# Attention over 32 units: the second softmax scaling of a run issued at the fifth filler product in place of the eighth

## The chip, the core and the metric

The kernel runs on one core of one Trainium2 chip. The metric is device time in microseconds: the median of three executions of the kernel before is 997.88 us (997.6 to 998.34). A second source is one execution taken by the hardware profiler, with its own time and its own span.

## The reference

One layer of a hybrid encoder trunk: RMSNorm, one input projection, two-dimensional neighbourhood attention, a SiLU gate, one output projection with the residual, and a last RMSNorm. The sequence is 2048 tokens, laid out as 32 rows of 64; the width is 1024, in 16 heads of 64.

```python
h = rmsnorm(x, norm_0)
q, k, v, gate = jnp.split(h @ w_in_0, 4, axis=-1)      # 1024 -> 4 * 1024
# for every row r of 64 queries: keys and values of 8 rows, 16 columns around the query
s = jnp.einsum('bnqhd,bknjhd->bhnqkj', qr, kr) * 64 ** -0.5
s = jnp.where(col_valid, s + bias, -1e30)              # bias from rpb_0, per head
p = softmax(s)                                         # over the 8 rows and their columns
o = jnp.einsum('bhnqkj,bknjhd->bnqhd', p, vr)
x = x + (o * silu(gate)) @ w_out_0
out = rmsnorm(x, norm_f)
```

## The kernel before, in words

All matrices are float32. A product of two of them is made of three matmuls on TensorE: each operand is split into a leading part and a rest (`h` and `l` in the names: `hh`, `hl`, `woh`, `wol`, `gh`, `gl`), and the rest-by-rest product is left out. A split is two instructions: ScalarE (ACT) copies the operand to the leading part, then VectorE (DVE) subtracts that from the operand. A **filler product** below is one such matmul of 128x512, three of them for each block of 128 of the contraction.

The kernel has four stages. The first two make the values and most of the queries, keys and gates (seven products for a two-by-two block product, in place of eight). The third is the attention loop, in which all that the change touches stands. The fourth, `rows_by_seven`, makes six pairs of blocks of 128 output rows, again with seven products for a pair; the four blocks that come first are made plainly, by `outputs`, as filler in the loop.

**The loop (L1805).** There are 33 runs, m = 0 to 32. A unit of attention is a pair of heads `p` and a block `T` of eight query rows (512 queries). Run m makes the scores of unit m and finishes unit m - 1. A unit has two halves, of two column groups each: `scores(2m)` and `scores(2m + 1)`. The order of the work is fixed when the program is written out, by hand and by a counter of filler products (`clock`); each engine takes its instructions in that order and waits for semaphores. In one run TensorE (PE) has, in this order:

- filler products, which `feed` takes from the projections that are left (`pp`, L392 to L396) and, from about run 18, from the plain output rows (`po`, L1580 to L1584);
- 44 transposes of the probabilities of unit m - 1 (`turns`, L1357), from the tiles `x` to PSUM tiles `ph`; DVE and ACT copy these, three copies each, to `pta` (L1345, L1347);
- 32 score matmuls of unit m (`scores`, L1297) into PSUM tiles `s`, which can be written only when a PSUM bank has come free: the pool `banks` has eight, all kinds of PSUM tile share them, and nearly all the scores' banks are those that the `ph` copies empty;
- 32 value matmuls of unit m - 1 (`values`, L1376) into `o`.

Behind the scores, DVE adds the bias and takes the row minimum (L1306) and ACT takes the exponential and its sum (L1312). `normalise` then makes the reciprocals of four sums (L1317, DVE) and scales four tiles `x` by them. The first half of a unit is scaled inside `scores(2m + 1)`, by GpSimd (POOL) alone. The **second half is scaled in the next run**, `normalise(2 * m - 1, True, ...)`, so that its exponentials have time: there DVE scales two tiles (L1322), ACT one (L1324) and POOL one (L1326). The transposes read all of them.

Beside this, the loop issues:

- `consume`: the next split of a weight block, of `w_in` or, from about run 12, of `w_out` (L198 and L199: `woh`, `wol`). Before it, it asks for a load some blocks ahead (L171, SyncE's (SP's) queue), and it splits only a block that was asked for at least 36 counts earlier. Its place in a run is with the scaling (`between`) or ahead of the k-th part of the filler, by the run's number;
- `split_rows`: the split of a block of attention output for the plain output rows (L1422, L1423: `gh`, `gl`);
- `give`: what follows the last filler product of a projection's group. A gate's block goes through ACT (L372, tanh) and DVE (L373), `sg<-sg,pp`; a key's goes through ACT (L378);
- `add_rows`: the residual of an output block (L1452, DVE), and five counts later its squares (L1455, ACT, `xr<-y`);
- stores and loads on SP's queue that `store` has put down for a later count (`due`).

The lines in run m that set where the second scaling stands:

```python
a = amount[m] - 8
begin(m)
feed(8)
if m:
    ...
        normalise(2 * m - 1, True)
    ...
    for k in range(3):
        ...                      # split_rows() or consume(1, turn=True), by m and a
        feed(a * 0.2)
else:
    feed(a * 0.6)
feed(a * 0.4, 8 if a > 12 else 4)
if m:
    turns(m - 1)
```

`amount[m]` is 13.5 filler products, 1.5 more or less in runs 8 to 23. The last `feed` also runs on, by up to three products, while an event (a split, the end of a group) is less than 4 or 8 counts old.

Of the kernel before, what the change touches and what calls it, by code (L numbers as in the profile page):

```python
# [77 lines left out]
def build(ctx, tc, x, xr, xt, wg, bias, w_out, n0, nf, out):  # L78
# [191 lines left out]
    for n, (k, j, ph, c) in enumerate(halves):  # L270
        a = (KINDS[k] + j, ph)
# [36 lines left out]
    def consume(n, asked=False, turn=False):  # L308
        for _ in range(n):
            load_ahead()  # L310
            if attending[0] and not asked and not turn:
                return
            if state["used"] == len(items) or not may_use(items[state["used"]]):
                return
            if attending[0] and now() - asked_at[items[state["used"]]] < 36 and not asked:
                return
            it = items[state["used"]]
            state["used"] += 1
            use_item(it)
# [24 lines left out]
    def due(n):  # L344
        clock[0] += n
        while later and later[0][0] <= clock[0]:
            later.pop(0)[2]()
# [848 lines left out]
    def projections():  # L1196
        for n, (kind, j, ph, c) in enumerate(halves):
            state["half"] = n
            w = (KINDS[kind] + j, ph)
            for a in range(2):  # L1200
                if n == len(halves) - 5 and a == 0:
                    for k in range(RES_EARLY):
                        load_res(*turns_[k])
                if n == len(halves) - 1:
                    if a == 0:
                        load_og(0)
                        load_og(1)
                    else:
                        store(("og0",), 9, lambda: split_og(0))
                consume(1)  # L1210
                p = yield from group(w, a, c, n)
                state["event"] = clock[0]
                give(kind, 2 * j + a, c, p, True)
            state["done_halves"] = n + 1
# [100 lines left out]
    def normalise(i, both=False, between=None):  # L1315
        st = ST.pop(i)
        nc.vector.reciprocal(st[:, 8:12], st[:, 4:8])  # L1317
        for j, C in enumerate(pairs[i][2]):
            for s in range(2):
                o = 8 + 2 * j + s  # L1320
                if both and j:
                    nc.vector.tensor_scalar(X[i, C][s], X[i, C][s], st[:, o:o + 1], None, op0=OP.mult)  # L1322
                elif both and s:
                    nc.scalar.activation(X[i, C][s], X[i, C][s], AF.Copy, scale=st[:, o:o + 1])  # L1324
                else:
                    nc.gpsimd.tensor_scalar(X[i, C][s], X[i, C][s], st[:, o:o + 1], 1.0, op0=OP.mult, op1=OP.mult)  # L1326
        if between:
            between()
# [182 lines left out]
    def run_roots(most=99):  # L1511
        while roots and most and (roots[0][0] <= clock[0] or ended[0]):
            most -= 1
            _, n, root, scale, send = roots.pop(0)
            root()
            rooted.append((n, scale, send))

    def run_scales():
        while rooted:
            n, scale, send = rooted.pop(0)  # L1520
            scale()
            store(("y", n), 18, send)
# [7 lines left out]
    def rows_due():  # L1530
        n = ready["split"]
        return (n < ready["loaded"] and "turn" in ready and place[n] <= ready["turn"] + 3 and now() - late["loaded_at"][n] >= 40 \
                and sum(1 if hasattr(g, "rearrange") else 2 for g in G.values()) <= 6)

    def split_rows():
        n = ready["split"]
        if rows_due():
            split_og(n)
            ready["split"] += 1
            return True  # L1540
# [77 lines left out]
    def land_T2():  # L1618
        for f in ("A21", "A22"):
            load_rows_of(1, f, vh)  # L1620
        for m in range(LEADERS):
            load_rest_of(m)
        land([("T2", k, i) for k in range(4) for i in range(2)], [a[k, 1] for k in range(4) for a in (woh, wol)])
        for f in ("A21", "A22"):
            load_rows_of(2, f, qp)
# [11 lines left out]
    def form_rows(m, P):  # L1637
        src = A[m, uses[P][0]]
        F[m, P] = t = wp([128, 2, 512], F32R, "f")
        nc.scalar.activation(t[:, 0], src, AF.Copy)  # L1640
        nc.vector.tensor_tensor(t[:, 1], src, t[:, 0].bitcast(F32), OP.subtract)
# [108 lines left out]
    for m in range(8, 24):  # L1750
        amount[m] += 1.5 if m % 2 == 0 else -1.5
    calm_debt = 3
    amount += [(96 * (12 - len(units_two)) + 48 * PLAIN - sum(amount) - first - end_of_it) / (cycles - 25)] * (cycles - 25) + [end_of_it]
    fill = projections()
    outs = outputs()
# [3 lines left out]
    def feed(n, calm=0):  # L1759
        credit[0] += n  # L1760
        while credit[0] > 0 or credit[0] > -calm_debt and clock[0] - state["event"] < calm:
            if alive[0]:
                got = next(fill, None)
                if got is None:
                    alive[0] = False
                    continue
            else:
                got = next(outs, None)
                if got is None:
                    due(max(credit[0], 0.0))  # L1770
                    credit[0] = min(credit[0], 0.0)
                    return
            credit[0] -= got
            due(got)
# [5 lines left out]
    def all_loads():  # L1780
        while any(e[1][0] == "load" for e in later):
            later.pop(0)[2]()

    def begin(m):
        all_loads()
        quiet[0] = False
        if m >= 1:
            later_loads([lambda: load_sg(*order[m - 1])], 1, 0)
        if m == cycles - 1:
            later_loads([land_first], 1.5, 0)  # L1790
            later_loads([lambda f=f, i=i: load_rows_of(i, f) for i in ((2, 0, 1) if PLAIN <= 6 else (0, 1)) for f in ("A11", "A12")], 10, 0.5)
        if m == cycles:
            later_loads([land_rest], 4, 0)
        if m < cycles:
            later_loads([lambda: load_v(*order[m])], 4, 0)
        if m + 1 < cycles:
            nx = order[m + 1]
            later_loads([load_q(*nx), load_k(*nx)], 7, 5)
            if (nx[0], ROW_TYPE[nx[1]]) not in EM:
                later_loads(load_bias(nx[0], ROW_TYPE[nx[1]]), 3, 1.5)  # L1800
# [4 lines left out]
    for m in range(cycles + 1):  # L1805
        a = amount[m] - 8
        begin(m)
        feed(8)
        if m:
            due_here = []  # L1810
            quiet[0] = True
            if a < 12 and m > 8 and m % 2:
                normalise(2 * m - 1, True, lambda: due_here.append(split_rows() or consume(1, turn=True)))
            else:
                normalise(2 * m - 1, True)
            most, behind = 99 if a > 12 else 0 if rows_due() else 1, bool(rooted)
            run_scales()
            if not (behind or any(due_here)):
                run_roots(most)
            for k in range(3):  # L1820
                if m == 1 and k == 2:
                    pass
                elif a > 12 or not any(due_here) and (k < 1 or k < 2 and m > 8 and m % 2 == 0):
                    got = split_rows()
                    due_here.append(got)
                    if not got:
                        consume(1, turn=True)
                    elif a < 12 and m % 2 == 0 and len(items) - state["used"] == 8:
                        feed(a * 0.2)
                        consume(1, turn=True)  # L1830
                feed(a * 0.2)
        else:
            feed(a * 0.6)
        quiet[0] = False
        feed(a * 0.4, 8 if a > 12 else 4)
        if m:
            turns(m - 1)
        if m == cycles:
            all_loads()
            feed(6)  # L1840
            while next(outs, 0) != 0:
                due(1)
            land_T2()
            for n in range(3):
                form_rows(n, 1)
        else:
            scores(2 * m)
            if m == 0:
                feed(first)
            scores(2 * m + 1, lambda: normalise(2 * m))  # L1850
            if m == 0:
                consume(2, turn=True)
        if m:
            values(m - 1)
        runs[0] += 1
        if m == 8:
            late_loads()
# [37 lines left out]
```

## Time and profile before

| | |
|---|---|
| median of three runs | 997.88 us (997.6 to 998.34) |
| profiled execution, its own time | 998.06 us |
| its span | 996.0 us (2.1 us less than its time) |
| TensorE (PE) busy | 986.9 us, 99% |
| weight loads (PEld) busy | 789.4 us, 79% |
| VectorE (DVE) busy | 772.9 us, 78% |
| ScalarE (ACT) busy | 541.6 us, 54% |
| GpSimd (POOL) busy | 128.5 us, 13% |
| mean granted TensorE clock | 0.999 |

The first transposes of the loop start at 575.28 us of the span (run 1), the last at 871.33 us (run 32). From 875.30 us to the end it is `rows_by_seven`. TensorE is busy all the time by the page, but its matmuls overlap, and a short wait between two of them hardly shows in that row; the time from the first matmul of a block to the first of the next tells it better. Weight loads have a row of their own.

### The profile page before, as it was taken

What the parts mean: (1) busy time and instruction counts of PE and PEld (TensorE: products, weight loads), DVE (VectorE), ACT (ScalarE), POOL (GpSimd) and SP (SyncE); (2) the same over time, 40 slices, a digit from 0 to 9 for tenths busy, and PEclk for the clock granted to TensorE, in tenths of its full rate; (3) what the DMA queues carried; (4) which work ended last, traced back from release to release, by engine and by line L of the source; (5) the groups of instructions that cost most, each with busy time, mean ns of one, the idle gap of its engine ahead of it and who ended that gap; (6) DMA issues with size and microseconds to landing.
All of it is one profiled execution on the core that took longest, in us unless ns stands there. A gap on an engine that the chain in (4) does not pass through costs nothing.

```text
span 996.0 us, 19496 instructions
## 1 busy us (share of the span) xinstructions
PE 986.9 (99%) x6892; PEld 789.4 (79%) x6892; DVE 772.9 (78%) x1703; ACT 541.6 (54%) x1310; POOL 128.5 (13%) x204
## 2 busy tenths in 40 slices
PE   9999999999999999999999999999999999999997
PEld 6888888888888888888888777777776777788886
DVE  5899888987665876766776687788889888886866
ACT  7863245465535442333433377777777786653443
POOL 0000001231100000000000022223232322201110
PEclk9999999999999999999999999999999999999999
DMA  8933547777947846656565798888978787997754
GB/s 285 347 116 104 195 134 255 246 250 251 363 150 222 275 123 194 205 174 213 175 191 195 229 286 270 271 240 261 320 231 290 244 251 236 329 358 199 196 153 116
DMA packets 150120, 227.65 MB, mean 229 GB/s; under 512 B 13640, under 2 KB 65096, under 8 KB 150024
## 3 DMA queue, kind: packets, MB, share of 16 engines
q1 hardware_dynamic: 147000, 221.30, 69.1%
q0 software_dynamic: 2592, 4.72, 2.9%
q8 instruction: 54, 0.88, 0.4%
q10 hardware_dynamic: 432, 0.40, 0.1%
q14 instruction: 42, 0.34, 0.1%
HBM read 160.31 MB, written 66.06 MB: 227 GB/s over the span
## 4 chain that ended last, share of the span: by engine, by line
PE 97%; ACT 1%; DVE 1%; DMA 0%; SPq 0%; issue 0%; POOL 0%; DVEq 0%; POOLq 0%
PE pp L448 40%; PE pv L614 13%; PE py L1674 11%; PE o L1376 8%; PE s L1297 7%; PE ph L1357 4%; PE pp L394 3%; PE pp L396 2%; PE pp L392 2%; PE pv L729 2%; PE po L1582 1%; PE po L1584 1%; PE po L1580 1%; DMA land<-in_xt_dram 0%; ACT x L1312 0%; DVE pta L1345 0%
## 5 line engine op out<-in xcount | busy, mean ns | idle before, releaser
L448 PE MATMUL pp<-h,f 128*128 128x512 f32 x576 | 185.4, 389 | 0.0
L448 PE MATMUL pp<-t,f 128*128 128x512 f32 x702 | 171.3, 389 | 0.0
L448 PEld LDWEIGHTS pp<-t,f 128*128 128x128 f32 x702 | 131.8, 188 | 27.4
L1326 POOL TENSOR_SCALAR x<-x,st 128x360 f32<-128x360 f32 (+5 forms) x160 | 81.8, 527 | 526.2 <-DVE st L1317 526.2
L1312 ACT ACTIVATE x<-x,st 128x360 f32<-128x360 f32 (+5 forms) x256 | 134.2, 526 | 26.9 <-DVE st L1306 26.8
L448 PEld LDWEIGHTS pp<-h,f 128*128 128x128 f32 x576 | 108.1, 188 | 22.5
L448 PE MATMUL pp<-l,f 128*128 128x512 f32 x288 | 112.1, 389 | 0.0
L1306 DVE CUSTOM_DVE_ANT_0 x<-s,em 128x360 f32<-128x360 f32 (+5 forms) x256 | 102.7, 457 | 2.2 <-issue 0.7
L431 DVE TENSOR_TENSOR f<-raw,f 128x512 fp32r<-128x512 f32 x105 | 75.8, 726 | 19.9 <-ACT f L430 19.7
L1376 PEld LDWEIGHTS o<-pta,vt 120*64 120x64 f32 (+2 forms) x1024 | 68.7, 137 | 22.4 <-DVE st L1306 15.2
L430 ACT ACTIVATE f<-raw 128x512 fp32r<-128x512 f32 x105 | 63.6, 622 | 37.1 <-DVE raw L437 22.0
L1376 PE MATMUL o<-pta,vt 120*64 120x192 f32 (+5 forms) x1024 | 83.5, 316 | 0.0
L1297 PE MATMUL s<-kt,q 64*64 64x360 f32 (+5 forms) x1024 | 73.1, 413 | 0.4 <-DVE pta L1345 0.3
L1347 ACT ACTIVATE pta<-ph 120x512 f32<-120x512 f32 (+5 forms) x96 | 48.9, 556 | 33.8 <-PE ph L1357 33.7
L1345 DVE COPY pta<-ph 120x512 f32<-120x512 f32 (+5 forms) x96 | 56.0, 638 | 13.4 <-PE ph L1357 13.1
L448 PEld LDWEIGHTS pp<-l,f 128*128 128x128 f32 x288 | 54.0, 188 | 11.3
L1674 PE MATMUL py<-woh,f 128*128 128x512 f32 x192 | 60.9, 390 | 0.0
L614 PE MATMUL pv<-wh,t 128*128 128x512 f32 x176 | 56.2, 389 | 0.0
L1297 PEld LDWEIGHTS s<-kt,q 64*64 64x64 f32 x1024 | 36.5, 132 | 21.7 <-DVE pta L1345 4.9
L448 PE MATMUL pp<-sixths,f 128*128 128x512 f32 x198 | 52.7, 389 | 0.0
L1357 PEld LDWEIGHTS ph<-ident,x 64*120 64x120 f32 (+2 forms) x1408 | 42.6, 128 | 11.7 <-issue 10.6
L430 ACT ACTIVATE f<-s 128x512 fp32r<-128x512 f32 x42 | 26.2, 624 | 45.6 <-DVE s L437 40.4
(227 smaller groups left out, 1872.8 us busy)
## 6 DMA issues: line engine op xcount, KB each, us to landing
raw<-in_wg_dram SPq DMA_DIRECT2D x124, 256.0 KB, 5.1
row<-in_xr_dram SPq DMA_DIRECT2D x32, 256.0 KB, 5.4
vd<-v SPq DMA_DIRECT2D x32, 256.0 KB, 5.0
sgd<-sg SPq DMA_DIRECT2D x32, 256.0 KB, 3.2
q<-qd SPq DMA_DIRECT2D x32, 256.0 KB, 5.8
sgt<-sgd SPq DMA_DIRECT2D x32, 256.0 KB, 7.0
ogd<-og SPq DMA_DIRECT2D x32, 256.0 KB, 3.4
kt<-kd SPq DMA_DIRECT2D x16, 480.0 KB, 6.4
```

Source lines behind the costliest of these rows:

```text
L430: nc.scalar.activation(t[:, 0], src, AF.Copy)
L431: nc.vector.tensor_tensor(t[:, 1], src, t[:, 0].bitcast(F32), OP.subtract)
L448: nc.tensor.matmul(B[n, P], t[:, int(m == 2), c], x[k][int(m == 1)], start=P in (1, 6, 5) and k == 0 and m == 0, stop=k == 3 and m == 2, s ...
L614: nc.tensor.matmul(p, a[:, o], b, start=P in (1, 6, 5) and k == 0 and m == 0, stop=k == 3 and m == 2, skip_group_check=True)
L1297: nc.tensor.matmul(places[C, s][h * 64:h * 64 + 64], qt[a, g * 64:g * 64 + 64], kt[a, :r1 - r0, c0:c0 + 8 * WIDE[C]].rearrange("p r (s c) ...
L1306: nc.vector.tensor_tensor_reduce(X[i, C][s], pst[s], EM[p, ROW_TYPE[T]][C > 0][s], -1.0, 1e38, OP.add, OP.min, st[:, o:o + 1])
L1312: nc.scalar.activation(X[i, C][s], X[i, C][s], AF.Exp, bias=st[:, o:o + 1], scale=-1.0, accum_out=st[:, 4 + o:5 + o])
L1326: nc.gpsimd.tensor_scalar(X[i, C][s], X[i, C][s], st[:, o:o + 1], 1.0, op0=OP.mult, op1=OP.mult)
L1345: nc.vector.tensor_copy(o, i_)
L1357: nc.tensor.transpose(ph[b, h][:k, o:o + 64], X[2 * m + late_, group[g]][s][q, at:at + k], ident[q, q])
L1376: nc.tensor.matmul(o[s * 64:s * 64 + 64, g0 * 64:g1 * 64], vt[:k, strip, s * 64:s * 64 + 64], t[:k, n * 64:(n + g1 - g0) * 64], start=stri ...
L1674: nc.tensor.matmul(B[m, P], t[:, a, c], b, start=P in (1, 6, 5) and k == 0 and i == 0, stop=k == 3 and i == 2, skip_group_check=True)
```

## The change

The count at which a run's second scaling is issued goes from eight filler products to five (`HEAD`). What was issued with it or behind it comes along: the first split of the run, the roots and scales of output rows. The three products go to the first part of the filler behind it, so that a run's filler keeps its sum. All counts that other work is put down for stay; so where a gate's end, a square, a store or a load used to be due between the fifth and the eighth product, it now stands behind the scaling and not ahead of it.

```diff
+    HEAD = 5
...
-        feed(8)
+        feed(HEAD)
         if m:
...
-                feed(a * 0.2)
+                feed(a * 0.2 + (8 - HEAD if k == 0 else 0))
         else:
-            feed(a * 0.6)
+            feed(a * 0.6 + 8 - HEAD)
```

## The prediction

> **What bounds the kernel now.** I read the page's first and fourth parts, then the table of who waited for whom, then the score blocks of single runs.
>
> ```profile
> PE 986.9 (99%) x6892; PEld 789.4 (79%) x6892; DVE 772.9 (78%) x1703; ACT 541.6 (54%) x1310; POOL 128.5 (13%) x204
> PE 97%; ACT 1%; DVE 1%; DMA 0%; SPq 0%; issue 0%; POOL 0%; DVEq 0%; POOLq 0%
> PEld s L1297 <- DVE pta L1345: 4.9, 12, 0.7
> ```
>
> TensorE sets the end: 99% busy, 97% of the chain that ended last. The change removes no matmul, so it can pay only where TensorE waits in the attention loop. The last row names the one wait there that comes from the softmax side: scores (L1297) wait for DVE's copies of the transposed probabilities (L1345). It counts 12, three in each of four runs. The score blocks of those runs, from the first score matmul to the first value matmul, stand below run 11's, which has no such wait. The columns are the stretch and its length, then the busy time (and count) of PE, PEld, DVE, ACT and POOL, granted clock, DMA share and GB/s.
>
> ```profile
> 668.08:670.46 2.38, 2.38 (x36) 1.14 (x33) 2.38 (x9) 1.78 (x7) 0.00 (x0) 1.00 1.01 312
> 678.06:681.48 3.42, 3.14 (x37) 1.21 (x33) 3.42 (x12) 1.94 (x6) 0.00 (x0) 1.00 1.02 285
> 746.92:750.18 3.26, 3.26 (x35) 1.41 (x32) 3.26 (x11) 1.78 (x6) 0.00 (x0) 1.00 0.77 214
> 767.13:770.09 2.96, 2.90 (x36) 1.03 (x32) 2.96 (x11) 1.48 (x5) 0.00 (x0) 1.00 0.92 250
> 786.99:789.97 2.98, 2.91 (x37) 1.03 (x33) 2.98 (x11) 1.49 (x5) 0.00 (x0) 1.00 0.91 227
> ```
>
> The same 32 matmuls take 2.38 us in run 11 and 3.42, 3.26, 2.96 and 2.98 us in runs 12, 19, 21 and 23: 1.04, 0.88, 0.58 and 0.60 us more, 3.10 us in all. In run 19 the transposes stall as well, at a tile that POOL scales:
>
> ```profile
> 676.62 1.51 PE L1357 MATMUL ph<-ident,x 64*120 64x64 f32 x44
> 744.92 0.56 PE L1357 MATMUL ph<-ident,x 64*120 64x64 f32 x11
> 745.78 1.21 PE L1357 MATMUL ph<-ident,x 64*120 64x64 f32 x33 [0.30 <-POOL x L1326]
> ```
>
> From its first transpose to its first score run 12 takes 678.06 - 676.62 = 1.44 us, run 19 takes 746.92 - 744.92 = 2.00: 0.56 us more. So what can be had is 3.10 + 0.56 = **3.66 us**, 0.37% of the time.
>
> **The change part by part.** Nothing but the order on each engine changes, and most runs keep it. First, why run 12 stalls.
>
> ```profile
> 673.75 0.19 ACT L1312 ACTIVATION_READ_ACCUMULATOR x<-x,st 128x1 f32 x1
> 674.46 0.60 ACT L372 ACTIVATE sg<-pp 128x512 f32<-128x512 f32 x1 [0.52 <-PE pp L396]
> 675.09 0.69 DVE L373 SCALAR_TENSOR_TENSOR sg<-sg,pp 128x512 f32<-128x512 f32 x1 [1.28 <-ACT sg L372]
> 675.70 0.17 DVE L1317 RECIPROCAL st<-st 128x4 f32<-128x4 f32 x1
> 675.90 1.04 DVE L1322 TENSOR_SCALAR x<-x,st 128x360 f32<-128x360 f32 x2
> 676.06 0.68 POOL L1326 TENSOR_SCALAR x<-x,st 128x360 f32<-128x360 f32 x1 [2.06 <-DVE st L1317]
> 676.24 0.60 ACT L1324 ACTIVATE x<-x,st 128x360 f32<-128x360 f32 x1 [1.18 <-DVE st L1317]
> 676.74 1.14 ACT L198 ACTIVATE woh<-raw 128x512 fp32r<-128x512 f32 x2
> 677.39 1.29 DVE L199 TENSOR_TENSOR wol<-raw,woh 128x512 fp32r<-128x512 f32 x2 [0.44 <-ACT woh L198]
> 678.60 1.75 DVE L1345 COPY pta<-ph 120x384 f32<-120x384 f32 x3
> ```
>
> The last exponential's sum is ready at 673.94. DVE could make the reciprocals then, but the gate's `sg` (L373) stands ahead, which waits for ACT's tanh and so for the filler group's end. That costs 1.76 us; behind it come the scalings, two splits, and at last the copies, at 678.60, which is 1.98 us behind the first transpose. The place in DVE's order, run 12 before, from the end of the last unit to the first copy of transposes:
>
> ```order
> L1380 TENSOR_TENSOR og<-o,sgt 128x512
> L373 SCALAR_TENSOR_TENSOR sg<-sg,pp 128x512
> L1317 RECIPROCAL st<-st 128x4
> L1322 TENSOR_SCALAR x_7151<-x_7151,st 128x360
> L1322 TENSOR_SCALAR x_7152<-x_7152,st 128x360
> L199 TENSOR_TENSOR wol<-raw,woh 128x512 x2
> L1345 COPY pta<-ph_7221 120x6x64
> ```
>
> and the same stretch now:
>
> ```order
> L1380 TENSOR_TENSOR og<-o,sgt 128x512
> L1317 RECIPROCAL st<-st 128x4
> L1322 TENSOR_SCALAR x_7151<-x_7151,st 128x360
> L1322 TENSOR_SCALAR x_7152<-x_7152,st 128x360
> L373 SCALAR_TENSOR_TENSOR sg<-sg,pp 128x512
> L199 TENSOR_TENSOR wol<-raw,woh 128x512
> L1345 COPY pta<-ph_7215 120x6x64
> ```
>
> The scaling overtakes the gate, and one of two splits leaves the run. With the durations above: reciprocals 673.95 to 674.12, scalings to 675.2; ACT scales to 674.8 and makes the tanh to 675.3; `sg` ends at 676.0; one split (half of 1.14 on ACT, half of 1.29 on DVE) ends by 676.7. How late may DVE then start its copies? The other stalled runs tell:
>
> ```profile
> 747.30 1.75 DVE L1345 COPY pta<-ph 120x384 f32<-120x384 f32 x3
> 765.69 1.51 PE L1357 MATMUL ph<-ident,x 64*120 64x64 f32 x44
> 767.22 1.75 DVE L1345 COPY pta<-ph 120x384 f32<-120x384 f32 x3
> 785.55 1.51 PE L1357 MATMUL ph<-ident,x 64*120 64x64 f32 x44
> 787.09 1.75 DVE L1345 COPY pta<-ph 120x384 f32<-120x384 f32 x3
> 756.39 0.39 PE L1357 MATMUL ph<-ident,x 64*120 64x64 f32 x6
> 757.02 1.76 DVE L1345 COPY pta<-ph 120x384 f32<-120x384 f32 x3 [0.38 <-PE ph L1357]
> ```
>
> The copies start 1.98, 2.38, 1.53 and 1.54 us behind the first transpose in runs 12, 19, 21 and 23; less the loss of each (1.04, 0.56 + 0.88, 0.58, 0.60) that leaves 0.94, 0.94, 0.95 and 0.94. So **0.94 us is free and all beyond it is lost one for one**. Where DVE is idle, as in run 20, the copies start after 0.63 us. In run 12 DVE is now free before 676.62 + 0.63: the loss of 1.04 us goes. What is late next there is PE itself.
>
> Run 19 has run 12's order before; now the gate stands behind the scaling and no split is left in the run. Its last sum:
>
> ```profile
> 742.74 0.18 ACT L1312 ACTIVATION_READ_ACCUMULATOR x<-x,st 128x1 f32 x1
> ```
>
> Reciprocals from 742.92, scalings to 744.2, `sg` to 744.9; POOL's tile, 0.16 us behind DVE's first and 0.68 long as in run 12, to 744.0. The transposes start at 744.92 with all tiles scaled. All of 0.56 + 0.88 = 1.44 us goes.
>
> Run 21, ACT's order before, from the last exponential on (`xr<-y` are the squares of an output block, `gh` the split of an attention block):
>
> ```order
> L1312 ACTIVATE x_8709,st<-x_8709,st 128x360
> L1455 ACTIVATE xr,st_8740<-y 128x512
> L1324 ACTIVATE x_8698<-x_8698,st 128x360
> L1422 ACTIVATE gh<-ograw 128x512 x2
> L1347 ACTIVATE pta<-ph_8779 120x6x64
> ```
>
> and now:
>
> ```order
> L1312 ACTIVATE x_8704,st<-x_8704,st 128x360
> L1324 ACTIVATE x_8693<-x_8693,st 128x360
> L1422 ACTIVATE gh<-ograw 128x512 x2
> L1455 ACTIVATE xr,st_8734<-y 128x512
> L1347 ACTIVATE pta<-ph_8774 120x6x64
> ```
>
> ```profile
> 764.33 1.04 DVE L1322 TENSOR_SCALAR x<-x,st 128x360 f32<-128x360 f32 x2
> 764.87 0.58 ACT L1324 ACTIVATE x<-x,st 128x360 f32<-128x360 f32 x1
> 766.01 1.29 DVE L1423 TENSOR_TENSOR gl<-ograw,gh 128x512 fp32r<-128x512 f32 x2 [0.64 <-ACT gh L1422]
> ```
>
> The square moves behind the split, so ACT scales when DVE does, at 764.33 in place of 764.87. DVE, idle 0.64 us for `gh`, starts `gl` and so the copies 0.54 earlier: 0.99 behind the first transpose, a loss of 0.05 in place of 0.58. Gain 0.53 us.
>
> Run 23 keeps DVE's and ACT's order. But PE's filler shifts by a product between some neighbouring runs: run 22 has one fewer, run 23 ten for nine. PE's order before, the last fillers of run 23 (`po`, plain output rows) and its first transpose:
>
> ```order
> L1580 MATMUL po<-woh,gh 128x512
> L1582 MATMUL po<-woh,gl 128x512
> L1584 MATMUL po<-wol,gh 128x512
> L1580 MATMUL po<-woh,gh 128x512
> L1357 MATMUL ph_9127<-ident,x_9027 120x64
> ```
>
> and now:
>
> ```order
> L1582 MATMUL po<-woh,gl 128x512
> L1584 MATMUL po<-wol,gh 128x512
> L1580 MATMUL po<-woh,gh 128x512
> L1582 MATMUL po<-woh,gl 128x512
> L1357 MATMUL ph_9124<-ident,x_9023 120x64
> ```
>
> One more product stands ahead of the transposes. A filler product's step:
>
> ```profile
> 665.87 0.39 PE L394 MATMUL pp<-l,w 128*128 128x512 f32 x1
> 666.10 0.39 PE L396 MATMUL pp<-h,w 128*128 128x512 f32 x1
> ```
>
> The transposes come 0.23 us later against the copies; of 0.60, 0.37 stays. **Sum: 1.04 + 1.44 + 0.53 + 0.23 = 3.24 us.**
>
> Costs. One `w_out` split more stands in each of runs 16, 20 and 25, about 0.65 us on DVE. In runs 16 and 25 DVE idles longer than that ahead of its copies:
>
> ```profile
> 716.89 1.16 DVE L1345 COPY pta<-ph 120x384 f32<-120x384 f32 x2 [1.35 <-PE ph L1357]
> 805.62 0.55 DVE L1345 COPY pta<-ph 96x384 f32<-96x384 f32 x1 [1.20 <-PE ph L1357]
> ```
>
> In run 20 it idles 0.38 (above), and one filler product more puts the transposes 0.23 later: 0.04 beyond the cover, far inside 0.94. I take 0 for the three; 0.65 each is the upper end. A key's copy (run 3) and a square (run 30) also fall behind the scaling, on ACT, with no loss there to mend or make: 0. SP's queue: some weight loads move ahead of `q` and `kt` loads whose unit is a run away: 0. In run 32 two output stores now stand ahead of the six loads that the last stage begins with:
>
> ```profile
> 863.30 3.91 SPq L1635 DMA_DIRECT2D raw<-ogd  x6
> raw<-ogd SPq DMA_DIRECT2D x24, 256.0 KB, 6.5
> 873.93 2.18 ACT L1640 ACTIVATE f<-raw 128x512 fp32r<-128x512 f32 x4
> ```
>
> Six issues take 3.91 us, so two more push them by 1.3. The first block read is the third of them: issued near 864.6, landed 6.5 us on at 871.1, read at 873.93. Slack 2.8 us: 0, with 1.3 as the upper end.
>
> There is another reading of the waits. By PE's own busy time the stalled blocks are idle for 0.28 + 0.06 + 0.07 = 0.41 us (length less busy), with 0.30 at the transposes 0.7 us, and the sum would be 0.7 at the most, 997.2 us, within 0.2%. I don't take it, because the blocks' lengths have the same 32 matmuls in them. The Trainium skill, Perfetto Trace Analysis, section Identifying the Most-Contended Engine, says that matmul busy time misleads since matmuls are pipelined, and that weight loads should be looked at. The trace agrees: PEld idles 3.42 - 1.21 = 2.21 us in run 12's block and 1.24 in run 11's, 0.97 more, near the block's 1.04.
>
> **The rivals.** (0.2%, 2.0 us, is about what a measurement tells from no change.)
>
> - *Only runs 12 and 19 are mended.* What runs 21 and 23 gain hangs on tenths of a microsecond in ACT's and PE's order; without it 1.04 + 1.44 = 2.48 us are left: 995.4 us. Against it: both orders are fixed, as shown.
> - *The last stage's loads come late.* The stores' 1.3 us reach TensorE: 994.64 + 1.3 = 995.94 us. Against it: 2.8 us of slack.
> - *The moved splits give it back*: three times 0.65, 1.95 us, if the cover is gone: 996.6 us. Against it: the idle rows.
> - *The scaling doesn't move in time*, since DVE is held by the exponentials' sums: so it is in most runs, which keep their order. If it holds in runs 12 and 19 too, the time stays at 997.9 us. Against it: in run 12 the sums were there at 673.94, 1.76 us before the reciprocals.
> - *Slower: a split's block has not landed.* A split is taken 36 counts after its load is asked for, 36 x 0.23 = 8.3 us.
>
> ```profile
> raw<-in_w_out_dram SPq DMA_DIRECT2D x16, 256.0 KB, 6.5
> ```
>
> Loads land after 6.5 us in the median. With the issue order changed, ACT could stand at a `woh` with the copies queued behind it. It decides from 8.3 + 0.94 = 9.2 us to landing, and to be slower by 2.0 us it must take back 5.2: a landing after 14.4 us, over twice the median. From there on the time is 999.9 us or more. Against it: no split in the loop waits for its load in this trace's rows above (L198's row in run 12 has no wait).
>
> **How the numbers follow.** The forecast has 0.68: 997.88 - 3.24 = 994.6 us (the profiled execution's own 998.06, 2.1 outside its span, would give 994.8; it lies 0.18 above the median). Its own range is 994.2 to 995.1. The rivals in order have 0.11, 0.06, 0.06, 0.04 and 0.05. Low end: the 0.42 that I leave goes too, from the fastest run, 997.6 - 3.66 = 993.9. High end 996.3: it takes in the first two rivals and leaves out 0.15. More than 2.0 us below 997.88 lie the forecast and the first rival, 0.79; within 2.0 us the next three, 0.16; above, the last, 0.05.
>
> **What would show it.** Right: the score blocks of runs 12 and 19 at 2.38 us, run 21's near 2.4, run 23's near 2.75; run 19's 44 transposes in one stretch; `sg` behind L1322 on DVE. Wrong: a wait of L1297 or L1357 in runs 16, 20 or 25, of L1640 for `raw`, or of L198 for its load; or score blocks as short as foreseen and the span no shorter.

## The result and the profile after

The changed kernel takes 994.99 us (median of eight executions, 993.93 to 995.79); the kernel before, on the same chip, 997.86 us. The ratio is 0.9968, with a 95% interval of 0.9958 to 0.9979: faster by 2.9 us. In two later rounds on the chip the same code, and a variant of it that changes one load, took 994.30 and 994.32 us. The forecast was 994.6.

The profiled execution of the changed kernel has a time of its own of 995.23 us and a span of 993.1 (before: 998.06 and 996.0). From its page, the busy times and the shares of the chain that ended last; from its table of who waited for whom, the one wait of TensorE's matmuls in the attention loop, and the row of its weight loads that the prediction started from:

```profile
PE 985.0 (99%) x6892; PEld 789.6 (80%) x6892; DVE 774.3 (78%) x1703; ACT 542.2 (55%) x1310; POOL 127.3 (13%) x204
PE 97%; DMA 1%; ACT 1%; DVE 0%; issue 0%; SPq 0%; DVEq 0%
PE s L1297 <- DMA kt<-kd: 0.9, 1, 0.9
PEld s L1297 <- DVE pta L1345: 1.0, 3, 0.4
```

Among the matmuls' waits neither the copies' (L1345) nor POOL's (L1326) is left. Among those of the weight loads the wait for the copies has gone from 4.9 us in twelve to 1.0 in three; the three are in run 23. A new wait is there: scores that wait 0.9 us for a load of keys (`kt`). The score blocks of runs 11, 12, 19, 21 and 23, in the columns of the prediction:

```profile
667.76:670.14 2.38, 2.38 (x36) 1.13 (x32) 2.38 (x9) 1.78 (x7) 0.00 (x0) 1.00 1.02 328
677.74:680.12 2.38, 2.38 (x36) 1.14 (x32) 2.38 (x9) 1.78 (x7) 0.00 (x0) 1.00 0.98 258
745.82:748.20 2.38, 2.38 (x37) 1.13 (x33) 2.38 (x9) 1.78 (x7) 0.00 (x0) 1.00 0.93 272
765.32:767.70 2.38, 2.38 (x36) 1.19 (x32) 2.38 (x10) 1.51 (x5) 0.00 (x0) 1.00 0.97 258
784.60:787.35 2.75, 2.75 (x36) 1.03 (x32) 2.75 (x10) 1.49 (x5) 0.00 (x0) 1.00 0.90 225
```

Three are as short as run 11's, and run 23 keeps 0.37 us. That is 1.04, 0.88, 0.58 and 0.23 us less than before. The weight loads (PEld, second in the row) tell the same: in run 12 they are busy for 1.14 of 2.38 us, idle for 1.24 (run 11: 1.25), where 2.21 us were idle before. The timeline of VectorE in run 12, from the reciprocals to the copies:

```profile
673.65 0.18 DVE L1317 RECIPROCAL st<-st 128x4 f32<-128x4 f32 x1 [0.16 <-ACT x L1312]
673.87 1.04 DVE L1322 TENSOR_SCALAR x<-x,st 128x360 f32<-128x360 f32 x2
674.98 0.69 DVE L373 SCALAR_TENSOR_TENSOR sg<-sg,pp 128x512 f32<-128x512 f32 x1
675.58 0.68 DVE L199 TENSOR_TENSOR wol<-raw,woh 128x512 fp32r<-128x512 f32 x1
676.94 1.76 DVE L1345 COPY pta<-ph 120x384 f32<-120x384 f32 x3 [0.67 <-PE ph L1357]
```

The reciprocals start when the last exponential's sum is there (they wait for ACT's L1312, no longer for the gate), the gate's `sg` stands behind the scaling, one split is left, and DVE is idle for 0.67 us until the first transposes give it something to copy. TensorE is late now, as foreseen. In TensorE's timeline the 44 transposes of run 19 are one stretch again, and scores follow 1.44 us behind; VectorE's copies in run 19 and, for the section on the prediction, both rows of runs 21 and 23 stand with it:

```profile
744.38 1.51 PE L1357 MATMUL ph<-ident,x 64*120 64x64 f32 x44
745.01 1.76 DVE L1345 COPY pta<-ph 120x384 f32<-120x384 f32 x3 [0.59 <-PE ph L1357]
...
763.88 1.51 PE L1357 MATMUL ph<-ident,x 64*120 64x64 f32 x44
764.83 1.75 DVE L1345 COPY pta<-ph 120x384 f32<-120x384 f32 x3
...
783.16 1.51 PE L1357 MATMUL ph<-ident,x 64*120 64x64 f32 x44
784.48 1.75 DVE L1345 COPY pta<-ph 120x384 f32<-120x384 f32 x3
```

What was not foreseen is in run 16. There the transposes are not late and the scores are. The timeline's row of SyncE for the load of `kt`, and TensorE's:

```profile
709.54 0.32 SPq L1236 DMA_DIRECT2D kt<-kd  x1
...
714.87 1.51 PE L1357 MATMUL ph<-ident,x 64*120 64x64 f32 x44
717.24 2.45 PE L1297 MATMUL s<-kt,q 64*64 64x240 f32 x32 [0.86 <-DMA kt<-kd]
```

The stretch from the first transpose to the first score is 2.37 us, 0.93 more than the 1.44 of an undisturbed run. The trace's semaphore events put the landing of `kt` at 717.10, 7.56 us after its issue and 0.14 ahead of the score. The same rows of the kernel before:

```profile
711.09 0.32 SPq L1236 DMA_DIRECT2D kt<-kd  x1
...
716.26 1.51 PE L1357 MATMUL ph<-ident,x 64*120 64x64 f32 x44
717.77 2.45 PE L1297 MATMUL s<-kt,q 64*64 64x240 f32 x32
```

There `kt` landed at 717.64, after 6.55 us, again 0.13 ahead of the score: it was the last to come before, too, at a cost of 0.07 us (a stretch of 1.51). Added over all 32 runs, the stretches of transposes and of scores are 114.69 us before and 112.26 after, 2.43 us less: 3.29 that the four runs gave and 0.86 that run 16 took (2.37 less 1.51). The first transposes of the loop also came 0.31 us earlier (574.97 for 575.28 us), which is within what this moment varies by in kernels that are the same up to there (574.42 to 575.28 us, see below). The two make 2.74 of the 2.83 us by which the span is shorter; the rest lies in the loop between the blocks, since from the last transposes to the end both kernels take 124.6 us.

### The profile page after: what moved, and what is told of

The parts are those of the page before. It is cut to its first block, busy times and chain, and to the rows that moved or that the text cites. A ratio compares the mean times of both kernels' runs of the same rounds, so it can differ in the third digit from the quotient of the medians.

```text
span 993.1 us, 19498 instructions
## 1 busy us (share of the span) xinstructions
PE 985.0 (99%) x6892; PEld 789.6 (80%) x6892; DVE 774.3 (78%) x1703; ACT 542.2 (55%) x1310; POOL 127.3 (13%) x204
## 4 chain that ended last, share of the span: by engine, by line
PE 97%; DMA 1%; ACT 1%; DVE 0%; issue 0%; SPq 0%; DVEq 0%
PE pp L448 40%; PE pv L614 13%; PE py L1674 12%; PE o L1376 8%; PE s L1297 6%; PE ph L1357 4%; PE pv L729 2%; PE pp L394 2%; PE pp L392 2%; PE pp L396 2%; PE po L1584 2%; PE po L1582 2%; PE po L1580 2%; DMA kt<-kd 1%; DMA vt<-vd 1%; ACT x L1312 0%
## 5 line engine op out<-in xcount | busy, mean ns | idle before, releaser
L1326 POOL TENSOR_SCALAR x<-x,st 128x360 f32<-128x360 f32 (+5 forms) x160 | 81.5, 524 | 524.0 <-DVE st L1317 524.0
L1312 ACT ACTIVATE x<-x,st 128x360 f32<-128x360 f32 (+5 forms) x256 | 134.1, 525 | 24.7 <-DVE st L1306 24.6
L1297 PE MATMUL s<-kt,q 64*64 64x360 f32 (+5 forms) x1024 | 70.8, 412 | 0.9 <-DMA kt<-kd 0.9
L1345 DVE COPY pta<-ph 120x512 f32<-120x512 f32 (+5 forms) x96 | 56.1, 638 | 13.3 <-PE ph L1357 13.0
L1297 PEld LDWEIGHTS s<-kt,q 64*64 64x64 f32 x1024 | 36.2, 132 | 20.2 <-DVE pta L1345 1.0
```

Source lines behind the costliest of these rows:

```text
L1297: nc.tensor.matmul(places[C, s][h * 64:h * 64 + 64], qt[a, g * 64:g * 64 + 64], kt[a, :r1 - r0, c0:c0 + 8 * WIDE[C]].rearrange("p r (s c) ...
L1312: nc.scalar.activation(X[i, C][s], X[i, C][s], AF.Exp, bias=st[:, o:o + 1], scale=-1.0, accum_out=st[:, 4 + o:5 + o])
L1345: nc.vector.tensor_copy(o, i_)
```

## The experiments

What had to be told apart: whether the four stalls and nothing else make the gain, and whether each is worth what its block shows; what the scaling and what the moved splits contribute; and where the wait in run 16 comes from. In the diffs, `-` and `+` are against the kernel named. "Stretch" is the time from a run's first transpose to its first score.

**The parts of the change, first round** (the kernel before: 998.63 us). Two kernels divide the change by runs:

```diff
# run12, against the changed kernel (ahead of feed(HEAD))
+        HEAD = 5 if m == 12 else 8
# not12, against the changed kernel
+        HEAD = 8 if m == 12 else 5
```

> Only run 12 has its second scaling at the fifth filler product, all others at the eighth; PE's filler counts are those of before, and SP's queue in run 15 is in the order of before. Theory A (TensorE's lead meets a saturated DMA queue): run 12's score block falls from 3.42 to 2.38 us, and what is gained comes back as a wait for the keys (kt) ahead of run 16's scores, 0.08 + 1.04, about 0.9 to 1.1 us; so nearly no gain, 997.6 to 998.0 us. Theory B (the keys come late because a w_out load stands ahead of them on SP's queue in the changed kernel): no such wait beyond before's 0.08 us, gain 1.0 us, about 996.8. Runs 19, 21 and 23 stay at 3.26 (and 2.00 for the transposes), 2.96 and 2.98 by both.

> All runs but run 12 have the second scaling at the fifth filler product; SP's queue in run 15 is in the order of the changed kernel. Theory A: run 12's score block stays at 3.42 us, TensorE has no lead by run 16 and the wait for kt there is 0.1 us or less. Theory B: the wait for kt is about 0.9 us as in the changed kernel. Both: run 19 at 1.44 and 2.38 us, run 21 at 2.38, run 23 at 2.75; gain 2.2 us by A, 1.3 by B: 995.7 or 996.5 us.

run12 took 997.93 us, ratio 0.9996 (0.9981 to 1.001); not12 995.54 us, ratio 0.9971 (0.9954 to 0.9987). In their profiles the blocks are as expected: in run12 only run 12's is mended (2.38 us), in not12 it stays at 3.42 and the others are mended. But run12's median shows no gain, and not12's waits have a longer one for `kt`; its table of waits:

```profile
PE s L1297 <- DMA kt<-kd: 1.6, 1, 1.6
```

and TensorE's timeline in run 3 (the scores) and in run 16:

```profile
593.74 0.75 PE L1297 MATMUL s<-kt,q 64*64 64x176 f32 x12 [0.23 <-ACT pta L1347]
...
716.00 1.51 PE L1357 MATMUL ph<-ident,x 64*120 64x64 f32 x44
719.08 1.24 PE L1297 MATMUL s<-kt,q 64*64 64x240 f32 x16 [1.56 <-DMA kt<-kd]
```

In run 16 of not12 theory A had foreseen a wait of at most 0.1 us and theory B about 0.9; neither came. So a mended run 12, which brings TensorE earlier to run 16, isn't what makes that wait: it is largest in the kernel that mends the other runs only, and 0.04 us (a stretch of 1.48) in the one that mends run 12. Whether it goes with the loads' changed order on SP's queue, which not12 shares with the changed kernel there, or comes by chance, these two leave open; the second round asks that. The division of the time was inconclusive here: run12's ten executions spread over 5 us (996.06 to 1001.13), and not12's median is 3.1 us below the kernel before, more than the 2.2 or 1.3 expected. It was done again below.

Two kernels divide the change by what is moved: the scaling alone, with runs 12 and 19 given their two splits back, or the splits alone, with the scaling left at the eighth product:

```diff
# scale_alone, against the changed kernel (behind the feed in the k loop)
+                if m == 12 and k == 1 or m == 19 and k < 2:
+                    consume(1, turn=True)
# splits_alone, against the kernel before
-                normalise(2 * m - 1, True, lambda: due_here.append(split_rows() or consume(1, turn=True)))
+                normalise(2 * m - 1, True, lambda: due_here.append(split_rows() or m == 19 or consume(1, turn=True)))
...
-                if m == 1 and k == 2:
+                if m == 1 and k == 2 or m == 12 and k == 0:
```

> The changed kernel with the splits put back: two in run 12 and two in run 19, as before, and none more in runs 16, 20 and 25; the scalings stay ahead of the gate's sg. If the gate ahead of the scaling was the cause, run 12's score block is 2.38 us with two splits as well (copies free at about 0.6 us behind the first transpose), and run 19, with one filler product more (13), is within 0.1 us of unstalled (copies 0.95 to 1.0 behind, limit 0.94). Run 21 at 2.38, run 23 at 2.98 (nine fillers again). Time 0.3 to 0.6 us above the changed kernel's if its wait for kt in run 16 stays. The rival, that the split leaving the run is what pays: run 12's block 0.6 us or more over 2.38, run 19's about 1 us over.

> The kernel before (second scaling at the eighth product) with only the splits moved as in the changed kernel: one in run 12, none in run 19, one more in runs 16, 20 and 25. By the limit of 0.94 us: run 12's copies start 1.38 us behind the first transpose, its score block is 2.38 + 0.44 = 2.82 us. Run 19's transposes still wait for POOL's tile, 2.00 us, and its scores are 2.4 to 2.5. Run 21 stays at 2.96; run 23 (ten fillers) 2.75. Sum 1.7 us less waiting, less what a kt wait in run 16 takes (A: 0.6 us): 996.2 to 996.8 us. The rival, that the lost splits alone explain the gain: 2.38 in both runs, time as the changed kernel's.

scale_alone took 996.54 us, ratio 0.9982 (0.9967 to 0.9997); splits_alone 996.36 us, ratio 0.9978 (0.9968 to 0.9989). Both were expected slower than the whole change; their medians lie 2.1 and 2.3 us below the kernel before of their round, with over 1 us to either side, too near each other to divide the time between scaling and splits. The blocks tell more. Run 12's score block in scale_alone, by stretches as above:

```profile
678.11:680.49 2.38, 2.38 (x37) 1.13 (x33) 2.38 (x9) 1.78 (x7) 0.00 (x0) 1.00 0.94 246
```

and in splits_alone, with the first transposes and the copies ahead of it:

```profile
677.61:680.43 2.82, 2.82 (x37) 1.03 (x33) 2.82 (x11) 1.49 (x5) 0.00 (x0) 1.00 0.97 258
676.17 1.51 PE L1357 MATMUL ph<-ident,x 64*120 64x64 f32 x44
677.55 1.75 DVE L1345 COPY pta<-ph 120x384 f32<-120x384 f32 x3
```

Copies 1.38 us behind the first transpose and a block of 2.82 us are what the bound of 0.94 us had foretold for splits_alone.

The scaling alone mends runs 12 and 19 with both splits in place, and run 21 to within 0.05 us; run 23 stays at 2.98. The splits alone leave 0.44 us in run 12, run 19's transposes stalled (a stretch of 2.00 us), and run 21 at 2.91; run 23 goes to 2.76. So in runs 12, 19 and 21 the scaling is enough by itself. The splits by themselves would do part of it, 0.60 of 1.04 us in run 12 and 0.88 of 1.44 in run 19; run 23 is theirs alone, by the filler product that they shift. Each part alone also costs something that the whole doesn't: scale_alone's block in run 28 is 0.53 us longer, splits_alone's in run 26 0.73. These two prices were not foreseen. In scale_alone's run 28 it is ACT that copies late:

```profile
829.26 1.43 PE L1357 MATMUL ph<-ident,x 64*96 64x64 f32 x44
830.35 0.63 ACT L1455 ACTIVATE xr<-y 128x512 f32<-128x512 f32 x1 [2.32 <-DVE y L1452]
830.98 1.44 ACT L1347 ACTIVATE pta<-ph 96x384 f32<-96x384 f32 x3
```

A square stands ahead of ACT's copies and waits 2.32 us for DVE's residual (L1452), so they start 1.72 us behind the first transpose, for 0.57 in the changed kernel. In splits_alone's run 26 it is DVE: a residual that waits 1.13 us for its filler group stands ahead of the scaling, as the gate does in run 12, and DVE's copies start 1.84 us behind. Added over all 32 runs, the stretches and blocks are 112.15 us in scale_alone and 113.64 in splits_alone, 2.54 and 1.05 less than in the kernel before: most of the gain is the scaling's.

**The wait for `kt` in run 16, second round** (the kernel before: 997.89 us). The changed kernel was run once more unedited (again), and with a load moved on SP's queue: either the second load of attention output, `ograw`, to behind `kt`, or `kt` itself ahead of all of them (there `q`, which is put down with it, also moves, from count 7 to 10):

```diff
# og_late, against the changed kernel
-                        load_og(1)
+                        store(("og1",), 12, lambda: load_og(1))
# kt_first, against the changed kernel
-            later_loads([load_q(*nx), load_k(*nx)], 7, 5)
+            later_loads([load_q(*nx), load_k(*nx)][::-1 if m == 15 else 1], 5 if m == 15 else 7, 5)
```

> The changed kernel once more, nothing edited: how much of what it lost in run 16 belongs to the program and how much to one execution. There its transposes-to-scores stretch took 2.37 us, 0.86 of it at kt<-kd, which landed 7.56 us after its issue. Theory 'order' (the changed order on SP's queue puts kt late): the same wait again, 0.7 to 1.0 us at PE s L1297 <- DMA kt<-kd, and the time 2.8 to 3.0 us below the kernel before. Theory 'landing' (kt's issue-to-landing time varies between executions, 6.4 to 8.4 us in the five profiles so far, and run 16 has no slack for it in any of these kernels): a wait anywhere from 0 to 1.7 us, and the median time unchanged by it: ratio near 0.997. Score blocks of runs 12, 19, 21, 23 at 2.38, 2.38, 2.38, 2.75 us by both.

> The changed kernel, with the second of the two 512 KB loads of attention output (ograw) in run 15 put down for 12 counts later, so that kt and sgt of run 16 stand ahead of it on SP's queue. If the 512 KB ahead of kt cause its late landing (theory 'order' and theory 'landing' alike: both say that run 16's kt has no slack), kt is issued 1 to 3 us earlier, at 707 to 708.5 us in place of 709.54, and no wait for it is left in run 16: stretch of 1.44 to 1.51 us in place of 2.37, 0.7 to 0.9 us less than the changed kernel's profile, and at the median 0 to 0.9 us less. If the DMA engines and not the queue hold kt (their share is about 1.0 from 692 to 720 us), it lands as late as before and the wait stays within 0.3 us of the changed kernel's in this job.

> The changed kernel, with only run 16's kt load put down for count 5 of run 15 in place of 12: on SP's queue it passes two weight loads, a bias load, q and both ograw loads; no other engine's order changes. Expected by theory 'order' and theory 'landing': kt lands at least 3 us before run 16's first score, no row PE s L1297 <- DMA kt<-kd of run 16, time as og_late's. What passes later by it is ograw (first split from it some 20 us later) and q, which lands 6 to 7 us after its issue and is read with kt: if q takes over as the late one, a wait for q of up to 0.8 us stands in run 16 in place of kt's, and the time doesn't move.

again took 994.30 us, ratio 0.9964 (0.9952 to 0.9977); og_late 994.17, ratio 0.9957 (0.9944 to 0.9971); kt_first 994.16, ratio 0.9961 (0.9948 to 0.9973). The same program as the changed kernel shows in run 16:

```profile
714.70 1.51 PE L1357 MATMUL ph<-ident,x 64*120 64x64 f32 x44
716.25 2.45 PE L1297 MATMUL s<-kt,q 64*64 64x240 f32 x32
```

A stretch of 1.56 us in place of 2.37. `kt` was issued at 709.38 and landed at 716.12: 6.74 us, for 7.56 in the other execution. The theory "order" falls, since the order is the same and the wait is 0.12 us, not 0.7 to 1.0. "Landing" stands: run 16 has no slack for `kt`, and what it costs depends on the execution. With `kt` ahead in SP's queue (kt_first), SyncE's row and TensorE's:

```profile
705.83 0.42 SPq L1236 DMA_DIRECT2D kt<-kd  x1
...
714.74 1.51 PE L1357 MATMUL ph<-ident,x 64*120 64x64 f32 x44
716.18 2.45 PE L1297 MATMUL s<-kt,q 64*64 64x240 f32 x32
```

`kt` lands at 711.41, 4.77 us ahead, the stretch is 1.44, and `q` didn't take over. og_late has 1.44 too (`kt` issued at 707.97, landed at 715.27, after 7.30 us). Both profiles are rid of the wait, and neither median is below again's by more than 0.25 us: a loss of 0.86 us isn't in again's median.

A fourth kernel tried for the last 0.37 us:

```diff
# best, against og_late
-                if m == 1 and k == 2:
+                if m == 1 and k == 2 or m == 23:
```

> og_late's kernel, and the split of run 23 left out there, so that a later run takes it. Run 23's copies of transposes then start early: its score block goes from 2.75 to 2.38 us, 0.37 us less than og_late, if no run that takes the split has its cover gone. With both, the changed kernel's time less 0.4 to 1.2 us. If the moved split gives it back where it lands (run 25 had 1.2 us of idle time ahead of its copies), a score block there is longer than 2.45 us and the time is og_late's.

It took 994.23 us, ratio 0.9958 (0.9945 to 0.9972), no better than og_late. Run 23's block is indeed 2.38 us, and run 25, which takes the split, is undisturbed (1.94 us, as the other runs there). But in its profile another `kt` came late, in run 3, at a cost of 0.24 us, and the loop began 0.45 us later than og_late's. Whether the 0.37 us is in the median can't be settled at this spread (993.63 to 994.9).

**The parts by runs again, with `kt` early, third round** (the kernel before: 998.16 us). The line of kt_first was put into the kernel before (before_kt), into run12 and into not12; whole_kt is kt_first's kernel once more.

> The kernel before, with run 16's kt load put down for count 5 of run 15 in place of 12. In the profiles of before the wait for this kt is 0 to 0.1 us, so by the theory that the whole gain comes from the stalls of runs 12, 19, 21 and 23 the time stays within 0.3 us of before: ratio 0.9997 to 1.0. By a rival, that part of the changed kernel's gain comes from its loads' order on SP's queue, the time falls by 0.5 us or more.

> Count 5 for the scaling in run 12 alone, eight in all other runs, and run 16's kt early, so that its landing can't hide the gain. Stalls theory: 1.04 us less than before, 996.85 by the earlier 997.89 us, ratio 0.9990; its score block in run 12 is 2.38 us, and those of runs 19, 21, 23 stay as before. Rival, by this kernel's earlier median (ratio 0.9996 with 0.9981 to 1.001): the microsecond saved in run 12 is lost again before the end, at another wait, and the time is before's; its place would show as a longer block behind run 12.

> Count 5 in all runs but run 12, and run 16's kt early. Stalls theory: 1.44 + 0.58 + 0.23 = 2.25 us less than before, 995.6 us, ratio 0.9977; run 12's score block stays at 3.42 us, no wait for kt in run 16 (the earlier profile of this kernel without the early kt had 1.63 us there). Rival, that the gains of single runs don't add: with run12_kt's they make less than 2.5 us together where whole_kt has 3.3.

> Count 5 in all runs, and run 16's kt early: the sum of the two parts. 1.04 + 2.25 = 3.29 us less than before, 994.6 us, ratio 0.9967, if the gains add; blocks of runs 12, 19, 21, 23 at 2.38, 2.38, 2.38, 2.75 us. In an earlier job the same kernel took 994.16 us at a before of 997.89.

| | median, us | ratio to before | less than before_kt, us | expected | all stretches and score blocks, us |
|---|---|---|---|---|---|
| before_kt | 997.84 | 0.9996 (0.9987 to 1.0004) | | | 115.83 |
| run12_kt | 996.74 | 0.9985 (0.9976 to 0.9994) | 1.10 | 1.04 | 113.59 |
| not12_kt | 995.10 | 0.9966 (0.9953 to 0.9978) | 2.74 | 2.25 | 112.37 |
| whole_kt | 994.32 | 0.9957 (0.9944 to 0.9969) | 3.52 | 3.29 | 111.32 |

The early `kt` alone takes 0.3 us from the median of the kernel before, with an interval from 1.3 us less to 0.4 more. The times alone so don't exclude half a microsecond from the loads' order; what an early `kt` could remove in the profile of before is 0.07 us. The two parts make 3.84 us together where the whole has 3.52. With about 1 us to either side of each they agree with adding, and the rival, less than 2.5 us together, is unlikely by the times; the blocks decide it, below. In the profiles run 12's block is 2.38 us in run12_kt:

```profile
677.20:679.58 2.38, 2.38 (x36) 1.13 (x32) 2.38 (x9) 1.78 (x7) 0.00 (x0) 1.00 0.90 244
744.90:748.17 3.27, 3.27 (x36) 1.42 (x33) 3.27 (x11) 1.79 (x6) 0.00 (x0) 1.00 1.02 252
```

with run 19's below it still long, and the other way round in not12_kt:

```profile
677.60:681.02 3.42, 3.14 (x37) 1.22 (x33) 3.42 (x12) 1.94 (x6) 0.00 (x0) 1.00 1.00 310
745.78:748.16 2.38, 2.38 (x37) 1.14 (x33) 2.38 (x9) 1.78 (x7) 0.00 (x0) 1.00 0.92 227
```

In before_kt's profile, run 20 has what run 16 had elsewhere:

```profile
755.91 1.51 PE L1357 MATMUL ph<-ident,x 64*120 64x64 f32 x44
758.58 1.85 PE L1297 MATMUL s<-kt,q 64*64 64x240 f32 x24 [1.16 <-DMA ogd<-og]
```

The wait is put down to `ogd<-og`. But that run's `kt` was issued at 749.17 and landed at 758.44, after 9.27 us and 0.14 ahead of the score, as in the other cases. Without this 1.23 us (2.667 less 1.438) before_kt's sum of stretches would be 114.60, and the three kernels would lie 1.01, 2.23 and 3.28 us below it: the sums of the blocks add, to 0.04 us.

## Why the prediction was right, and where it wasn't

- **The bound of 0.94 us.** It holds in places where it wasn't read off. Run 23's copies start at 784.48, 1.32 us behind its first transpose; less 0.94 that is 0.38, and its block is 0.37 too long. Run 21's copies start at 764.83, 0.95 behind; the 0.05 us left there by the forecast is not to be seen. The sum of four terms, 1.04 + 1.44 + 0.53 + 0.23, measured 1.04 + 1.44 + 0.58 + 0.23 = 3.29 for 3.24. The medians, 2.9 us in the first round and 3.6 to 3.8 in the later ones, lie on both sides of it and can't test the sum that finely; the blocks do. The bound is that of runs 9 to 23, whose tiles and score blocks are the largest. In run 28 of the kernel before, with smaller ones, DVE's copies start 1.24 us behind the first transpose and nothing is lost (a block of 1.94 us).
- **The other reading, by PE's own busy time**, at most 0.7 us, is out: the medians of the whole change, with `kt` moved or not, lie 2.9 to 3.8 us below those of the kernel before that they were timed with.
- **Run 12 needed only the scaling.** The forecast counted one split as gone and DVE free before the transposes. With both splits (scale_alone) the block is 2.38 as well.
- **Costs taken as nothing.** The splits of runs 16, 20 and 25: kt_first and whole_kt have all three, and stretches of 1.44, 1.44 and 1.36 us and blocks of 2.38, 2.38 and 1.94, those of undisturbed runs. The key's copy in run 3: the stretch is 1.36 us in the changed kernel as before. The stores in run 32: ACT's first read of `raw` (L1640) has no wait for a load, at 871.1 us for 873.9 before.
- **SP's queue, "a unit is a run away: 0".** This step was wrong, though its number for the change was near the truth. The change leaves `kt` of run 16 as much time as it had: from its issue to where the scores would start without it there are 6.61 us before (711.09 to 717.70) and 6.77 after (709.54 to 716.31). It has no slack in either, and 717.64 against 717.77 could have been seen in the trace of before. The loss of 0.86 in the profile is that execution's landing, not the order's price. The sign set for "wrong", a wait of L1297 in run 16, came, but from this load and not from the split that was suspected.
- **The rivals.** "Only runs 12 and 19" is ruled out by runs 21 and 23 in the rows above; "the scaling doesn't move" by DVE's row in run 12; the last stage's loads and the splits' return by the costs just named. That a split's block has not landed is ruled out by the changed kernel's table of waits, in which no `woh` (L198) waits for its load.

What the prediction takes from the Trainium skill (Perfetto Trace Analysis, Identifying the Most-Contended Engine) held in this sense: matmul busy time showed 0.41 us of stalls, and the weight loads' idle time went from 2.21 to 1.24 us in run 12's block while the block lost 1.04. It is no exact measure: in run 19's block the weight loads idled 3.26 - 1.41 = 1.85 us, 0.61 more than in run 11's, where 0.88 were lost.

What stays open: why the first transposes of the loop come between 574.42 and 575.33 us in the fourteen profiles (five of the kernels are the same up to run 12, and they alone spread over 574.42 to 575.28); and how often a late `kt` occurs, since each profile is one execution.

## What to carry to other kernels

An operation that waits for the end of a group and stands in an in-order engine's queue ahead of one whose inputs are ready holds up all behind it; look there before looking at durations. When a stall's cause is known in several places, solve them for one common bound (here 0.94 us of free lateness, for tiles of one size): it then gives the residue in places that are only half mended. And before a load is called hidden because it is issued a run early, compare its landing with its first use: 0.13 us of slack is none.

## What the runs showed of the hardware

- The load of `kt`, issued at the same place of the same program or nearly so, took 5.86 to 8.62 us to land in run 3 (352 KB) over the fourteen profiles, and 7.39 to 9.42 in run 20 (480 KB). In the two profiles of one program, the changed kernel and again, it was 6.72 and 6.09 us in run 3, 8.43 and 9.42 in run 20. No scores started less than 0.13 us behind its landing. They started 0.13 to 0.14 us behind it in up to two runs of a profile, and up to 1.63 us went there. The DMA engines were busy for a share of 0.94 to 0.99 in those parts (585 to 594, 703 to 718 and 745 to 758 us, in the profiles of the changed kernel, not12 and best). The share alone doesn't tell when a load comes late: kt_first, where none did, has 0.95, 0.98 and 0.99 there.
- Of the five such waits of over 0.15 us, the trace names `kt` for two. In run 3 of not12 and of best the trace names ACT's copies, 0.23 and 0.17 us, with `kt` landing at 593.61 and 593.87, 0.13 us ahead of the scores; ACT's copies start 0.57 us behind the first transpose there, as in the changed kernel, whose scores don't wait; in run 20 of before_kt it names a store of `og`.
